# The low-rank result in a tile of its own, not in the masks' scratch buffer

## The chip, the cores and the metric

The kernel runs as one program on one core of a Trainium2 chip. The engines are TensorE (PE, with its weight loads as PEld), VectorE (DVE), ScalarE (ACT), GpSimd (POOL) and SyncE (SP); each takes its own instructions in order, and they wait for each other through semaphores. The metric is the device time of one execution in microseconds (us). Three runs took 1478.11, 1479.92 and 1480.67 us, so the median before is 1479.92 us.

## The reference

One layer of a hybrid encoder, for 256 tokens of 2048 features in float32:

```
u      = rms_norm(x) @ w_in                       # 2048 -> 5408 columns
y_conv = conformer_conv(u[value], u[gate])        # 31 taps, 1024 channels
y_rwkv = rwkv7_time_mix(u[r, k, v, low-rank])     # 16 heads of 64, a recurrence over time
h      = x + concat(y_conv, y_rwkv) @ w_out
out    = rms_norm(h + moe(rms_norm(h)))           # 4 groups of 8 experts, top 1 and then top 2
```

The low-rank columns are the last 288 of w_in (64 for the decay, 64 for a, 160 for the gate). They are shifted by one frame with the mix `mu`, go through tanh or sigmoid, and are then multiplied by small matrices (`w_lora_up`, `a_lora_up`, `g_lora_up`) inside the time mix.

## The kernel before

**Stages.** The program has a front (norm, input projection, convolution, time mix, output projection), a short routing, and an expert stage of 16 pairs of experts, in which 400 MB of expert weights are read. The front keeps features on partitions: the normed input is held as two float32r parts, yh and yl (tiles yha, yhb, yla, ylb), and each 1 MB chunk of w_in, as it lands in the ring of six buffers w, is split on the chip into hi (ACT, line 246) and lo (DVE, line 247), four k-tiles at a time, into three rotating buffers each. A projection of 256 columns is two accumulators acc of 128 columns, and 16 k-tiles of three matmuls each (hi x yh, hi x yl, lo x yh, line 218), so 96 matmuls. The accumulators rotate through a PSUM pool of three banks (`pacc`).

**The beginning.** `norm_in` computes the low-rank columns first, before the norm's scale is known: 32 matmuls (line 314) of x times w_lo fill two banks of `pacc`, tiles la[0] and la[1], one for each half of the tokens. The scale rs is applied when they are evicted (line 376). Meanwhile ytmp, yh and yl are made (lines 342 to 344) and the first three splits. Then `small_loads` and `const_tiles` follow on DVE and POOL: some scaled parameters (lines 192 to 204), and the masks of the time mix, which are built in a scratch tile scr (lines 127 to 171). The scratch has the buffer with the tag "mix" in `ypool`, which has one buffer; ytmp has it before, and the tile mix (the convolution's output, eight blocks of 256 columns) has it after.

**`lora`** evicts la[0] and la[1] on ACT into lt (line 376), transposes three column ranges of each on PE (line 378, six transposes into three banks mm), shifts them (line 361 on ACT, 362 on DVE) into T1, G1 and G2, and applies tanh (lines 384, 386). T1 is first used in `rwkv_decay` and G1, G2 in `rwkv_out`.

**Behind it** stands `conv_duo(0)`: the gate projection (96 matmuls), its tanh sg from the two accumulators (line 645, ACT), the value projection (96 more), and UP = (sg + 1) x value (line 651, DVE), which frees the value's accumulators. Then come the convolution's 31 taps into mix (lines 656, 658), and `rwkv_duo(0)` with its projections of k, r and v. Fills of constant tiles from ident (line 722, ACT; line 719, DVE) stand in the same stretch.

**The order** of each engine's instructions is made by a list scheduler from the order of the code and priorities: loads and splits of a projection have a raised priority, the taps a lowered one. A tile that takes over a buffer waits for all that was done to the tile before it. The expert stage has its order on PE by hand; each weight chunk is loaded by SP (line 1095) when its slot is free.

Of the kernel before, what the change touches and what calls it, by code (L numbers as in the profile page):

```python
# [76 lines left out]
class Block:  # L77
# [293 lines left out]
    def lora(self):  # L371
        nc = self.nc
        ps = [self.bank(self.pmm, [128, 256], "mm") for _ in range(3)]
        for i in range(2):
            lt = self.mix[:, 2 * i:2 * i + 2].rearrange("p a b -> p (a b)")[:, 0:288]
            nc.scalar.activation(lt, self.la[i], AF.Copy, scale=self.rs[:, i:i + 1])
            for p, c in zip(ps, (0, 128, 160)):
                nc.tensor.transpose(p[:, 128 * i:128 * i + 128], lt[:, c:c + 128], self.ident)
        T1 = self.lo.tile([128, 256], F32, name="T1")
        G1 = self.lo.tile([128, 256], F32, name="G1")  # L380
        G2 = self.lo.tile([128, 256], F32, name="G2")
        for i, (p, t) in enumerate(zip(ps, (T1, G1, G2))):
            self.shift(p, self.mul_s[:, i:i + 1], self.omul[:, i:i + 1], t)
        nc.scalar.activation(T1[0:64], T1[0:64], AF.Tanh)
        for t in (G1, G2):
            nc.scalar.activation(t, t, AF.Tanh, scale=0.5)
            nc.vector.tensor_scalar(t, t, 0.5, 0.5, op0=OP.mult, op1=OP.add)
        self.T1, self.G1, self.G2 = T1, G1, G2
        self.tap("T1", T1)
# [902 lines left out]
```

## Time and profile before

| | |
|---|---|
| median of three runs | 1479.92 us |
| the profiled execution, its own time | 1477.63 us |
| its span | 1475.8 us |
| PE busy | 1398.8 us (95%) |
| DVE busy | 654.7 us (44%) |
| ACT busy | 416.1 us (28%) |
| POOL busy | 33.5 us (2%) |
| mean granted TensorE clock | 0.989 |
| DMA | 471.48 MB, mean 319 GB/s |

The span is from the first to the last instruction; the execution's own time is 1.8 us longer. Matmuls overlap, and their ends are modelled, so a busy PE is not a PE at its peak. Shares are means over stages with different limits: the front works on PE, DVE and ACT, the expert stage on PE and the DMA engines.

### The profile page before, as it was taken

The page shows a single profiled execution, that of the slowest core. Times are in us where ns is not written, and L with a number is a line of the kernel's source. Part 1 is how long each engine was busy: PE and PEld are TensorE (multiplying, and loading weights), DVE is VectorE, ACT ScalarE, POOL GpSimd, SP SyncE. Part 2 cuts the span into 40 slices and gives each one's busy share as a digit, 9 for nine tenths or more (in the row PEclk, how much of TensorE's full clock was granted, in tenths as well). Part 3 has the DMA queues.
Part 4 walks back from the last instruction along what each step waited for, and adds up shares of the span by engine and source line. Part 5 has one row for each costly group of instructions (what it writes and reads, how often), then busy time and mean ns, then how long its engine had stood idle before and what let it go on. Part 6 is the DMA issues. An engine that isn't in the chain of part 4 may idle for free.

```text
span 1475.8 us, 21342 instructions
## 1 busy us (share of the span) xinstructions
PE 1398.8 (95%) x8738; PEld 855.4 (58%) x8738; DVE 654.7 (44%) x1343; ACT 416.1 (28%) x770; POOL 33.5 (2%) x66
## 2 busy tenths in 40 slices
PE   6999999999999989999999999999999998999995
PEld 5989888989889954344344344344344343443432
DVE  6797986968967542232232232232231221312314
ACT  5657756676596330010010010000010000000102
POOL 5000000000000000000000000000000000000000
PEclk9999999999999999999999999999999999999997
DMA  7443332432537669999999999999999999999994
GB/s 279 145 150 115 110 131 88 149 118 76 179 129 290 280 250 371 425 424 425 424 422 426 425 424 422 426 424 425 425 424 425 424 426 424 423 426 425 422 424 155
DMA packets 68678, 471.48 MB, mean 319 GB/s; under 512 B 7984, under 2 KB 10096, under 8 KB 13280
## 3 DMA queue, kind: packets, MB, share of 16 engines
q1 hardware_dynamic: 67344, 467.96, 78.1%
q0 software_dynamic: 1088, 2.09, 0.6%
q8 instruction: 71, 1.16, 0.3%
q14 instruction: 31, 0.25, 0.0%
q10 hardware_dynamic: 144, 0.01, 0.0%
HBM read 467.93 MB, written 2.10 MB: 318 GB/s over the span
## 4 chain that ended last, share of the span: by engine, by line
PE 54%; DMA 30%; DVE 10%; ACT 2%; issue 1%; SPq 0%; ACTq 0%; DVEq 0%
DMA w<-in_w_up_dram 20%; PE acc L218 13%; DMA w<-in_w_down_dram 9%; PE y L218 9%; PE g L218 8%; PE u L218 8%; PE mm L218 7%; PE gt L218 5%; DVE lo L247 3%; PE cb L218 3%; DVE mix L658 2%; DVE MB L495 1%; PE cn L218 1%; ACT hi L246 1%; DVE xe L978 1%
## 5 line engine op out<-in xcount | busy, mean ns | idle before, releaser
L218 PE MATMUL u<-w,xe 128*64 128x512 f32 x1024 | 243.8, 593 | 10.8 <-DMA w<-in_w_up_dram 10.5
L218 PE MATMUL g<-w,xe 128*64 128x512 f32 x1024 | 241.3, 598 | 9.9 <-DMA w<-in_w_gate_dram 7.6
L218 PE MATMUL y<-w,hT 128*64 128x512 f32 (+1 forms) x1040 | 232.2, 594 | 0.7 <-ACT hT L1039 0.7
L1056 DVE TENSOR_TENSOR acc<-acc,cb 128x512 f32<-128x512 f32 (+1 forms) x130 | 86.3, 674 | 220.0 <-PE cb L218 220.0
L218 PEld LDWEIGHTS u<-w,xe 128*64 128x64 f32 x1024 | 75.7, 137 | 162.6 <-issue 138.6
L1031 DVE TENSOR_TENSOR hid<-sg,u 128x256 f32<-128x256 f32 x32 | 19.6, 613 | 322.7 <-PE u L218 322.7
L218 PEld LDWEIGHTS g<-w,xe 128*64 128x64 f32 x1024 | 72.0, 137 | 147.8 <-issue 127.2
L218 PEld LDWEIGHTS y<-w,hT 128*64 128x64 f32 x1040 | 70.7, 137 | 134.2 <-issue 118.1
L247 DVE TENSOR_TENSOR lo<-w,hi 128x1024 fp32r<-128x1024 f32 x108 | 127.5, 1180 | 47.0 <-ACT hi L246 34.3
L1027 ACT ACTIVATE sg<-g 128x512 f32<-128x512 f32 x16 | 9.6, 597 | 461.2 <-PE g L218 461.2
L218 PE MATMUL gt<-S,vt 128*128 128x128 f32 x1024 | 126.7, 280 | 6.7 <-DVE xe L978 5.2
L218 PEld LDWEIGHTS gt<-S,vt 128*128 128x128 f32 x1024 | 121.4, 195 | 15.0 <-DVE xe L978 8.7
L246 ACT ACTIVATE hi<-w 128x1024 fp32r<-128x1024 f32 x108 | 110.6, 1025 | 47.4 <-PE acc L218 44.0
L1069 ACT ACTIVATE yh<-y,gate 128x512 fp32r<-128x512 f32 (+1 forms) x65 | 44.3, 681 | 251.6 <-PE y L218 251.6
L658 DVE SCALAR_TENSOR_TENSOR mix<-UP,dw_s,mix 128x256 f32<-128x256 f32 x240 | 103.9, 476 | 2.6 <-ACT mix L656 2.4
L218 PE MATMUL acc<-yha,hi 128*128 128x256 f32 x320 | 92.3, 288 | 0.6 <-DVE rs L362 0.3
L218 PE MATMUL acc<-yla,hi 128*128 128x256 f32 x320 | 92.3, 288 | 0.0
L218 PE MATMUL acc<-yhb,lo 128*128 128x256 f32 x320 | 92.1, 288 | 0.0
L218 PE MATMUL acc<-yha,lo 128*128 128x256 f32 x320 | 91.8, 287 | 0.0
L218 PE MATMUL acc<-ylb,hi 128*128 128x256 f32 x320 | 91.4, 286 | 0.0
L218 PE MATMUL acc<-yhb,hi 128*128 128x256 f32 x320 | 90.4, 283 | 0.0
L978 DVE TENSOR_TENSOR xe<-gt,nffnp_s 128x512 f32<-128x512 f32 (+1 forms) x65 | 44.4, 683 | 85.6 <-PE gt L218 85.5
(354 smaller groups left out, 1907.1 us busy)
## 6 DMA issues: line engine op xcount, KB each, us to landing
w<-in_w_gate_dram SPq DMA_DIRECT2D x128, 1024.0 KB, 19.6
w<-in_w_up_dram SPq DMA_DIRECT2D x128, 1024.0 KB, 19.6
w<-in_w_down_dram SPq DMA_DIRECT2D x126, 1024.0 KB, 19.6
w<-in_w_in_dram SPq DMA_DIRECT2D x40, 1024.0 KB, 5.0
w<-in_w_out_dram SPq DMA_DIRECT2D x8, 768.0 KB, 4.6
w<-in_w_out_dram SPq DMA_DIRECT2D x6, 1024.0 KB, 5.1
xT_s<-in_xT_dram SPq DMA_DIRECT2D x4, 512.0 KB, 6.6
wlast<-in_w_out_dram SPq DMA_DIRECT2D x2, 1024.0 KB, 6.6
```

Of the source, the lines that this page charges most:

```text
L218: self.nc.tensor.matmul(*a, **k)
L246: nc.scalar.activation(hi, view, AF.Copy)
L247: nc.vector.tensor_sub(lo, view, hi.bitcast(F32))
L495: V.copy_predicated(MB[:, 2 * h + c], self.mkP.rearrange("p a b -> p (a b)"), P12[h])
L658: V.scalar_tensor_tensor(c, u, d, c, op0=OP.mult, op1=OP.add)
L978: self.nc.vector.tensor_mul(xe[:, a:a + n], ps, self.nffnp_s[:, k0:k0 + n, None].to_broadcast([128, n, 128]))
L1027: A.activation(sg, gp, AF.Silu)
L1031: V.tensor_mul(hid, *(t.rearrange("s (p f) -> s f p", f=4)[:, f:f + 2] for t in (sg, up)))
L1056: V.tensor_add(a, a, cb)
L1069: A.activation(yh, yp, AF.Copy, scale=gate)
```

## The change

The two evictions of the low-rank result no longer write to slices of mix. Each takes a tile of the tag "tl" in the pool `tmp`, of 128 x 512 floats in two buffers, whose first 288 columns are used. The tag is there already: `rwkv_mats` (line 511) takes tiles of it later for its transposes, by the same helper `lg`.

```diff
         for i in range(2):
-            lt = self.mix[:, 2 * i:2 * i + 2].rearrange("p a b -> p (a b)")[:, 0:288]
+            lt = self.lg("tl", (128, 4, 128)).rearrange("p a b -> p (a b)")[:, 0:288]
             nc.scalar.activation(lt, self.la[i], AF.Copy, scale=self.rs[:, i:i + 1])
```

Every engine has the same instructions as before (ACT's loads of its function tables stand elsewhere); the scheduler puts some of them in another order in the first part of the program, up to the k projection of `rwkv_duo(0)`. POOL's and SP's order is the same.

On PE, before: the end of the gate projection's first accumulator, as far as its splits are there (36 matmuls), the six transposes, and the second accumulator.

```order
L218 MATMUL acc<-yhb,hi 128x256
L218 MATMUL acc<-ylb,hi 128x256
L218 MATMUL acc<-yhb,lo 128x256
L378 MATMUL mm<-ident,mix 128x128 x6
L218 MATMUL acc<-yha,hi 128x256
L218 MATMUL acc<-yla,hi 128x256
L218 MATMUL acc<-yha,lo 128x256
```

On PE, now: the start of the gate projection.

```order
L218 MATMUL acc<-yha,hi 128x256
L218 MATMUL acc<-yla,hi 128x256
L218 MATMUL acc<-yha,lo 128x256
L378 MATMUL mm<-ident,tl 128x128 x3
L218 MATMUL acc<-yha,hi 128x256
L218 MATMUL acc<-yla,hi 128x256
L218 MATMUL acc<-yha,lo 128x256
L218 MATMUL acc<-yha,hi 128x256
L378 MATMUL mm<-ident,tl 128x128 x3
L218 MATMUL acc<-yla,hi 128x256
```

The transposes stood behind 36 gate matmuls, and now stand behind three and seven. The gate's two accumulators, which came one after the other for the first 36 matmuls each, now take turns at every split (12 matmuls each).

On ACT, before: from the last makings of yhb to the eviction of the low-rank result (DT and EP are the constant tiles of line 722).

```order
L343 ACTIVATE yhb<-ytmp 128x512 x4
L722 ACTIVATE DT_267<-ident 128x512
L722 ACTIVATE DT_268<-ident 128x512
L722 ACTIVATE EP_260<-ident 128x512
L722 ACTIVATE EP_261<-ident 128x512
L722 ACTIVATE EP_262<-ident 128x512
L722 ACTIVATE EP_263<-ident 128x512
L722 ACTIVATE EP_264<-ident 128x512
L722 ACTIVATE EP_265<-ident 128x512
L376 ACTIVATE mix<-acc,rs 128x288 x2
```

On ACT, now: from the first of these yhb on.

```order
L343 ACTIVATE yhb<-ytmp 128x512
L376 ACTIVATE tl<-acc,rs 128x288
L343 ACTIVATE yhb<-ytmp 128x512
L376 ACTIVATE tl<-acc,rs 128x288
L343 ACTIVATE yhb<-ytmp 128x512
L246 ACTIVATE hi<-w 128x1024
L343 ACTIVATE yhb<-ytmp 128x512
L722 ACTIVATE DT_267<-ident 128x512
L722 ACTIVATE DT_268<-ident 128x512
L722 ACTIVATE EP_260<-ident 128x512
L246 ACTIVATE hi<-w 128x1024
```

The evictions moved ahead of all eight fills, and the fourth split of the gate's weights and the first of the value's come between the yhb and the fills.

On ACT, before: the stretch from the shifts to the first sg.

```order
L361 ACTIVATE G_379<-mm,omul 128x256
L384 ACT_TABLE_LOAD
L384 ACTIVATE T_377<-T_377 64x256
L246 ACTIVATE hi<-w 128x1024
L386 ACTIVATE G_378<-G_378 128x256
L246 ACTIVATE hi<-w 128x1024
L386 ACTIVATE G_379<-G_379 128x256
L246 ACTIVATE hi<-w 128x1024
L645 ACTIVATE sg<-acc 128x256
```

On ACT, now: the same stretch, from the second to last piece of fills on.

```order
L246 ACTIVATE hi<-w 128x1024
L722 ACTIVATE EP_265<-ident 128x512
L361 ACTIVATE T_379<-mm,omul 128x256
L361 ACTIVATE G_380<-mm,omul 128x256
L361 ACTIVATE G_381<-mm,omul 128x256
L246 ACTIVATE hi<-w 128x1024
L645 ACT_TABLE_LOAD
L645 ACTIVATE sg<-acc 128x256 x2
L246 ACTIVATE hi<-w 128x1024
```

The two sg moved ahead of the tanh of T1, G1 and G2, and the table load stands before them. On DVE the lo of the same splits moved up likewise: one stands between the last two yl, and one each after the memset of line 131, after line 154, after the second piece of line 162 and after the shifts of line 362.

## Rows read from the trace of the kernel before

**Rows 1.** Page, busy tenths in 40 slices: PE.

```profile
PE   6999999999999989999999999999999998999995
```

**Rows 2.** PE's waits, whole span: us in total, times, longest us.

```profile
PE u L218 <- DMA w<-in_w_up_dram: 10.5, 10, 1.3
...
PE mm L378 <- ACT mix L376: 7.3, 1, 7.3
```

**Rows 3.** Busy time by stretch: PE, PEld, DVE, ACT, POOL; clock, DMA share, GB/s.

```profile
32.00:39.28 7.28, 0.00 (x0) 0.00 (x1) 6.75 (x39) 4.45 (x10) 4.39 (x14) 0.82 0.30 123
39.28:43.60 4.32, 4.32 (x21) 4.32 (x22) 1.39 (x4) 3.48 (x7) 0.00 (x0) 0.51 0.00 0
43.60:60.00 16.40, 16.40 (x141) 16.40 (x141) 9.08 (x10) 8.35 (x11) 0.00 (x0) 1.00 0.56 193
60.00:100.00 40.00, 38.67 (x313) 35.71 (x311) 39.37 (x83) 23.92 (x39) 2.14 (x4) 1.00 0.48 165
100.00:450.00 350.00, 339.10 (x3003) 308.57 (x3005) 284.26 (x556) 242.09 (x465) 9.66 (x18) 1.00 0.36 122
...
600.00:1000.00 400.00, 397.58 (x2022) 174.87 (x2022) 104.31 (x206) 28.07 (x43) 0.00 (x0) 1.00 1.01 424
```

**Rows 4.** Timeline of ACT, 26 to 80 us: start, us, instruction, idle before.

```profile
26.96 1.23 ACT L343 ACTIVATE yhb<-ytmp 128x512 fp32r<-128x512 f32 x2 [1.89 <-DVE ytmp L342]
...
32.69 3.21 ACT L722 ACTIVATE EP<-ident 128x512 f16<-128x512 f32 x6
38.73 0.89 ACT L376 ACTIVATE mix<-acc,rs 128x288 f32<-128x288 f32 x2 [2.83 <-DVE w L171]
40.43 0.47 ACT L361 ACTIVATE T<-mm,omul 128x256 f32<-128x256 f32 x1 [0.81 <-PE mm L378]
...
41.66 1.28 ACT L384 ACT_TABLE_LOAD   x1
...
43.27 1.04 ACT L246 ACTIVATE hi<-w 128x1024 fp32r<-128x1024 f32 x1
...
47.79 0.39 ACT L645 ACTIVATE sg<-acc 128x256 f32<-128x256 f32 x1 [0.47 <-PE acc L218]
```

**Rows 5.** Timeline of DVE, 26 to 80 us.

```profile
29.80 0.67 DVE L342 TENSOR_TENSOR ytmp<-y1a,mm 128x512 f32<-128x512 f32 x1
...
32.43 0.16 DVE L192 TENSOR_SCALAR omul<-mul_s 128x3 f32<-128x3 f32 x1
...
33.88 0.11 DVE L132 MEMSET scr<- 64x64 f32 x1
...
36.45 0.28 DVE L156 TENSOR_TENSOR scr<-scr 128x128 f32<-128x128 int32 x1
...
37.86 0.48 DVE L165 TENSOR_TENSOR mkB<-scr 128x128 uint8<-128x128 f32 x2
...
44.35 1.23 DVE L247 TENSOR_TENSOR lo<-w,hi 128x1024 fp32r<-128x1024 f32 x1 [2.14 <-ACT hi L246]
...
60.51 0.42 DVE L651 SCALAR_TENSOR_TENSOR UP<-sg,acc 128x256 f32<-128x256 f32 x1 [0.29 <-PE acc L218]
```

**Rows 6.** Timeline of PE, 0 to 110 and 31.5 to 100 us.

```profile
25.75 2.10 PE L314 MATMUL acc<-w,y1b 128*128 128x288 f32 x8
...
39.28 1.54 PE L378 MATMUL mm<-ident,mix 128*128 128x128 f32 x6 [7.33 <-ACT mix L376]
40.48 0.56 PE L218 MATMUL acc<-yha,hi 128*128 128x256 f32 x1
...
41.05 0.41 PE L218 MATMUL acc<-yha,lo 128*128 128x256 f32 x1
41.26 0.41 PE L218 MATMUL acc<-yha,hi 128*128 128x256 f32 x1
```

**Rows 7.** Waits of SP's DMA queue, 440 to 620 us.

```profile
SPq L1095 <- PE g L218: 39.2, 6, 13.2
SPq L1095 <- PE y L218: 20.7, 4, 10.4
```

## The prediction

> **What bounds the kernel now.** I read the page's slices first: TensorE (PE) is busy nine tenths or more in nearly every slice but the first [rows 1], so what matters in the front is where PE stands still. The list of PE's waits has one long wait there: the six transposes of line 378 wait 7.3 us, once, for the eviction of line 376. The waits for expert weights sum to more, but they are many short ones, the longest 1.3 us [rows 2]. The busy time by stretch shows what that one wait costs: from 32.0 to 39.28 us PE runs nothing while VectorE (DVE) is busy 6.75 of 7.28 us. Then from 39.28 to 43.6 PE's granted clock is 0.51, its 1.2 GHz level, and from 43.6 on it is 1.00, 2.4 GHz; PE had idled before it fell, and had worked again for 4.3 us before it rose [rows 3]. ScalarE (ACT) tells why: the eviction at 38.73 had stood 2.83 us behind DVE's tile w, line 171 [rows 4], the last instruction of the mask building. The lora tile was a slice of mix, mix takes over scr's buffer, and so the eviction had to wait for every mask. PE could not pass it by: two of the three acc banks held the low-rank result, and the second half of the first projection needs one of them.
>
> After 60 us PE and DVE are both nearly full up to 100 us (38.67 and 39.37 of 40), PE stays so to 450 us (339.1 of 350) at clock 1.00, and the expert stage runs on the DMA engines (share 1.01 at 424 GB/s from 600 to 1000) [rows 3].
>
> **The change, step by step.** The bytes, the instructions and the DMAs are the same; only the target of two evictions differs. The wait for the masks goes, and the scheduler then puts the two evictions behind the first and second yhb on ACT, the transposes between the first gate matmuls on PE, and the splits hi and lo (lines 246, 247) between the memsets and masks. Nothing moves on the queues of GpSimd and SyncE. From the k projection on, all engines have the same order as before, so the question is when that part begins. I take as its mark the second UP write on DVE (line 651), which waits for PE's last value matmul: 60.51 us before [rows 5].
>
> What is late next. I follow the new order with the old durations. The first yhb ends at 26.96 + 0.62 = 27.6, and the last eight low-rank matmuls end at 25.75 + 2.10 = 27.85, those of the first half about 0.25 earlier [rows 4, 6]. The evictions take 0.50 each with a yhb of 0.62 between them, so they end near 28.1 and 29.2. PE has three gate matmuls to do, waits about 0.2 for the first, and again about 0.2 for the second: 0.4 in all. The six transposes took from 39.28 to 40.5 at the half clock, so 0.1 each at the full one, and by 29.5 they are done with seven of the 96 gate matmuls. A matmul costs 16.40 / 141 = 0.116 us at the full clock [rows 3]; the other 89 end at 29.5 + 10.3 = 39.8.
>
> Then 23 value matmuls run into the bank of low-rank half two, until 42.5, and the 24th wants a bank that line 645 (sg) must free. ACT reaches that late: yhb at 30.5 behind its ytmp (29.80 + 0.67), hi at 31.5 when PE has done the first 24 gate matmuls, then yhb (0.6), three fills of line 722 at 3.21 / 6 = 0.53, hi (1.0), four fills, hi, one fill, the three shifts (40.43 to 41.66, 1.2), hi, the table load (1.28), sg (0.39): 31.5 + 1.05 + 0.6 + 1.6 + 1.0 + 2.1 + 1.0 + 0.5 + 1.2 + 1.05 + 1.28 + 0.39 = 43.3 [rows 4, 5]. PE waits 0.8 us there, where it now waits nothing. The remaining 73 value matmuls end at 43.3 + 8.5 = 51.8, with the drain of the last 52.1. Behind the waiting PE stand only these matmuls, and DVE and ACT wait for them.
>
> DVE's splits must be there in time, since each now stands behind a piece of mask work. The pieces last 32.43 to 33.9, to 36.45 and to 37.9 (1.4, 2.6 and 1.4 us); the last has 0.8 to 38.6 and then five instructions, two fills and three shifts, at about the 0.4 of a UP, 2.8 in all [rows 5]. With 1.23 for each lo, the four lo of the value projection end near 37.1, 40.9, 43.5 and 47.5, and PE wants them at 40.0, 41.4, 46.2 and 49.0: 2.9, 0.5, 2.7 and 1.5 us to spare. The second is the tight one.
>
> The sum:
> - the idle stretch: 7.3 us gone;
> - the half clock behind it: 1.2 GHz for 4.32 us costs (1 - 0.51) x 4.32 = 2.1 at most, and 14 matmuls at 0.21 instead of 0.116 cost 1.3 at least [rows 3, 6]. The transposes lie in that stretch too, so I take 1.9;
> - the two short waits for the evictions: -0.4;
> - the new wait for sg: -0.8.
>
> That is 8.0; the walk by itself gives 60.5 - 52.1 = 8.4. I take 8.2 us.
>
> Bounds, since nothing here was ever run in this order. Above: DVE's work between 32 and 60 us is 6.75 + 1.39 + 9.08 = 17.2 of 28 us [rows 3], so it can be squeezed by 10.8 us and no more. Below: if the mask work, from the second piece on (33.9 to the eviction at 38.73, 4.8 us) [rows 4, 5], were all to stand in the way of splits that PE waits for, 3.4 us would be left. I stay by the walk, whose spare times come from the nearest rows.
>
> Does the shift last to the end? What follows waits only for engines. SyncE's waits before expert weights are for PE and DVE to free slots (39.2 and 20.7 us on lines of PE are the largest) [rows 7], DMA has 0.36 of its time in use up to 450 us [rows 3], and the expert stage is so many bytes at one rate from its first free slot. So it starts 8.2 us earlier and ends 8.2 us earlier. On the profiled execution, 1477.63 us, that is 1469.4; the median of the runs is 2.3 us above it, and from 1479.92 I forecast 1471.7 us.
>
> A page speaks against the clock term. The Trainium skill, "TensorE: Matmul & The Clock Gate", section "A second HAM failure mode: psum-queue depth-cycling", says that short idles between matmul groups that cycle through PSUM banks can make the clock swing between its two levels. By that rule the new bank wait would bring back some of the 1.9 us or more; it is the third rival below. The trace bears it out little: between 100 and 450 us, where matmul groups share the same banks, the granted clock is 1.00.
>
> **Rivals.**
> - Masks in the way. If the lo with 0.5 us to spare is late, and those behind it too, PE waits for DVE instead of ACT. For it: a piece of mask work now stands ahead of each of these splits, and DVE takes its queue in order. Against it: DVE has 10.8 us idle in that stretch. It gives a gain of 3 to 5 us, 1475 to 1477.
> - Swallowed later. If the expert weights came from a stream that started by itself, an earlier front would only wait for them: 1479.9. For it: the DMA share of 1.01. Against it: the waits of rows 7 are all for engines. That the change doesn't free the eviction at all would give the same time; against that stands the order, in which the transposes come behind three gate matmuls instead of 36.
> - Slower, by the clock. If the many short waits between 27 and 52 us held PE at 1.2 GHz, the 192 matmuls of the first two projections would take 0.21 instead of 0.116: 192 x 0.094 = 18 us more, less the 7.3 + 1.9 that went, so 9 us slower, 1489. It decides from 8.2 / 0.094 = 87 matmuls at the half clock on. For it: the clock did fall once after PE stood still here. Against it: it fell in a stand of 7.3 us, and the new waits are 0.2 to 0.8.
>
> **How the numbers follow.** The forecast with gains of 5 to 10.8 us has 0.82; masks in the way 0.07; swallowed, or not done, 0.07; slower by the clock 0.04. A difference under 0.2% (3 us) can hardly be told from none here. Faster by more takes the forecast and most of the second, 0.88; within it 0.08; slower 0.04. The range runs from a gain of 10.8 us (1469.1) with a little of the runs' own spread (1478.11 to 1480.67), 1468.6, to 3.7 us, 1476.2; that leaves out the two last rivals and the weaker part of the masks' one.
>
> **What would show it.** In the changed profile the wait of line 378 for line 376 falls from 7.3 us to under 0.5; no stretch between 27 and 60 us has a granted clock of 0.5; PE waits near 42 us for sg, 0.4 to 1.2 us; the second UP write comes at 52 us; the first copies into MB and the first expert matmul come 8 us earlier, and the expert stage has its old length. It is wrong if PE waits for lo between 40 and 49 us, if the clock shows its lower level after 30 us, or if the shift at UP has shrunk by the time the expert stage ends.

## The result and the profile after

The first comparison gave 1468.93 us (four runs, 1466.81 to 1469.90) against 1479.99 us (four runs) on the same chip: ratio 0.9925, 95% interval 0.9908 to 0.9943. Two more comparisons of the same pair, told below, gave 0.9952 (0.9938 to 0.9965) and 0.9943 (0.9930 to 0.9956). By the ratios the three are 11.1, 7.1 and 8.4 us, and their intervals overlap; the forecast was a gain of 8.2 us, to 1471.7. The profiled execution took 1469.9 us with a span of 1467.9, against 1477.63 and 1475.8: 7.7 to 7.9 us. Why these numbers differ is the second half of this text. One reason lies in the kernel before: in the 57 executions of it in the later comparisons the median is 1477.0 us, and the four of the first comparison (1478.11 to 1480.67) all lie at the upper end of that spread (1475.23 to 1480.16), while the changed kernel's medians of the first and third comparison differ by 0.4 us only. Of the 57, all that took 1478 us or more had a mean granted clock of 0.986 or 0.987, and all under 1477.8 had 0.989 or 0.990. So some 3 us of the 11.1 most likely come from those four executions, and not from the change.

The page's slices of PE. The first digit has risen from 6 to 8; one other digit differs, that of the slice with the routing, which reads 7 for 8 [rows 1].

```profile
PE   8999999999999979999999999999999998999995
```

PE's waits over the whole span: us in total, times, longest. The wait of line 378 is no longer in the list [rows 2]; the new wait for sg is its last line. The waits for expert weights are what they were.

```profile
PE u L218 <- DMA w<-in_w_up_dram: 10.7, 9, 1.6
...
PE acc L218 <- ACT sg L645: 0.2, 1, 0.2
```

Busy time by stretch: PE, PEld, DVE, ACT, POOL; clock, DMA share, GB/s. The later stretches begin 8 us earlier than those of [rows 3], as the forecast would have them.

```profile
27.00:32.00 5.00, 5.00 (x43) 4.83 (x42) 4.33 (x6) 3.04 (x7) 5.00 (x10) 1.00 0.95 362
32.00:39.28 7.28, 7.28 (x64) 7.28 (x63) 6.61 (x25) 7.28 (x15) 4.64 (x12) 1.00 0.59 225
39.28:43.60 4.32, 4.10 (x35) 3.90 (x34) 4.32 (x18) 3.29 (x6) 0.12 (x1) 1.00 0.54 154
43.60:52.00 8.40, 8.40 (x73) 7.94 (x72) 7.13 (x16) 5.20 (x8) 0.00 (x0) 1.00 0.61 196
52.00:92.00 40.00, 37.37 (x308) 34.86 (x306) 39.66 (x83) 23.77 (x40) 2.15 (x4) 1.00 0.47 162
92.00:442.00 350.00, 340.04 (x3014) 309.26 (x3012) 283.72 (x555) 242.44 (x466) 9.69 (x18) 1.00 0.36 122
592.00:992.00 400.00, 397.58 (x2021) 174.81 (x2022) 104.05 (x206) 27.62 (x42) 0.00 (x0) 1.00 1.01 424
```

From 32.00 to 39.28 PE did nothing before and is now busy all the time; DVE builds the same masks in it. From 39.28 to 43.60 the clock is 1.00 where it was 0.51.

ACT, the stretch of the evictions and of sg (start, us, instruction, idle before). The evictions stand at 26.97 and 27.87 instead of 38.73, and the first sg (the tanh of the gate projection) at 41.94 [rows 4].

```profile
26.97 0.49 ACT L376 ACTIVATE tl<-acc,rs 128x288 f32<-128x288 f32 x1
27.35 0.62 ACT L343 ACTIVATE yhb<-ytmp 128x512 fp32r<-128x512 f32 x1
27.87 0.49 ACT L376 ACTIVATE tl<-acc,rs 128x288 f32<-128x288 f32 x1
...
40.65 1.28 ACT L645 ACT_TABLE_LOAD   x1
41.94 0.66 ACT L645 ACTIVATE sg<-acc 128x256 f32<-128x256 f32 x2
```

DVE, with the four lo of the value projection and the UP writes [rows 5]. The rs of line 331 is a mark that lies ahead of the change: it was at 17.79 before, so 0.5 us of every shift of a start below come from an earlier beginning of this one execution. The last row is the third UP write.

```profile
17.27 0.17 DVE L331 RECIPROCAL rs<-rs 128x2 f32<-128x2 f32 x1 [3.71 <-ACT rs L330]
...
35.38 1.23 DVE L247 TENSOR_TENSOR lo<-w,hi 128x1024 fp32r<-128x1024 f32 x1
...
39.24 1.21 DVE L247 TENSOR_TENSOR lo<-w,hi 128x1024 fp32r<-128x1024 f32 x1
...
41.80 1.21 DVE L247 TENSOR_TENSOR lo<-w,hi 128x1024 fp32r<-128x1024 f32 x1
...
45.57 1.21 DVE L247 TENSOR_TENSOR lo<-w,hi 128x1024 fp32r<-128x1024 f32 x1
...
50.44 0.96 DVE L651 SCALAR_TENSOR_TENSOR UP<-sg,acc 128x256 f32<-128x256 f32 x2
...
131.23 0.42 DVE L651 SCALAR_TENSOR_TENSOR UP<-sg,acc 128x256 f32<-128x256 f32 x1 [0.73 <-PE acc L218]
```

The same two marks in the trace of the kernel before:

```profile
17.79 0.17 DVE L331 RECIPROCAL rs<-rs 128x2 f32<-128x2 f32 x1 [4.11 <-ACT rs L330]
...
140.54 0.42 DVE L651 SCALAR_TENSOR_TENSOR UP<-sg,acc 128x256 f32<-128x256 f32 x1 [0.73 <-PE acc L218]
```

PE: the transposes stand in two threes among the first gate matmuls, and the only idle time that is left before the second UP is 0.22 us for sg [rows 6].

```profile
27.60 0.52 PE L378 MATMUL mm<-ident,tl 128*128 128x128 f32 x3
...
28.44 0.53 PE L378 MATMUL mm<-ident,tl 128*128 128x128 f32 x3
...
42.38 0.39 PE L218 MATMUL acc<-yha,hi 128*128 128x256 f32 x1 [0.22 <-ACT sg L645]
```

SP's waits before expert weights, 440 to 620 us, are still for PE to free slots [rows 7].

```profile
SPq L1095 <- PE g L218: 45.1, 8, 13.9
SPq L1095 <- PE y L218: 20.7, 4, 10.4
```

**Where the time went.** Two marks split the span. From rs to the third UP write (line 651; 140.54 before, 131.23 after) it is the front: 122.75 us before, 113.96 after, 8.8 less. From there to the last accumulation of line 1056 (1462.35 and 1455.14) it is the rest: 1321.8 before, 1323.9 after, 2.1 more. The shift is 9.3 us at the first copy into MB (97.10 to 87.79) and still 9.3 when ACT loads the function table for the experts' silu (line 1027, 536.30 to 527.01). It is 8.95 at the first expert matmul (538.91 to 529.96), 8.6 at the first silu itself (572.20 to 563.56) and 7.2 at the end. In the changed kernel:

```profile
527.01 1.28 ACT L1027 ACT_TABLE_LOAD   x1
...
563.56 0.60 ACT L1027 ACTIVATE sg<-g 128x512 f32<-128x512 f32 x1 [35.27 <-PE g L218]
```

The table load is only a mark of the routing's end; the expected text of the run with the routing filled, further down, counts it as a silu and so calls the first silu the second. The longer waits of PE there are alike in both traces; what differs is the clock, as the runs below show.

### The profile page after: what moved, and what is told of

The parts are those of the page before. It is cut to its first block, busy times and chain, and to the rows that moved or that the text cites. A ratio compares the mean times of both kernels' runs of the same rounds, so it can differ in the third digit from the quotient of the medians.

```text
span 1467.9 us, 21346 instructions
## 1 busy us (share of the span) xinstructions
PE 1398.4 (95%) x8738; PEld 854.9 (58%) x8738; DVE 654.4 (45%) x1343; ACT 415.5 (28%) x770; POOL 34.5 (2%) x66
## 4 chain that ended last, share of the span: by engine, by line
PE 58%; DMA 26%; DVE 11%; ACT 3%; issue 1%; ACTq 0%; SPq 0%; DVEq 0%
DMA w<-in_w_up_dram 18%; PE acc L218 12%; PE y L218 10%; PE g L218 9%; PE u L218 9%; DMA w<-in_w_down_dram 8%; PE mm L218 7%; PE gt L218 6%; DVE lo L247 3%; PE cb L218 3%; DVE mix L658 2%; DVE MB L495 1%; PE acc L314 1%; ACT hi L246 1%; PE cn L218 1%
```

## Experiments

Each front below is the time from rs to the third UP write in that run's trace, so that the start of the program is set equal; each shift is against the 122.75 us of before. Each ratio is against executions of the kernel before on the same chip.

**The pair again.** Without an edit.

> The changed kernel once more, against the kernel before on the same chip, in five rounds. The single pair of traces gave 7.7 to 7.9 us, the medians of the first runs 11.1 us with an interval of 8.4 to 13.6. Theory A (the gain is the front's shift at the second UP write, 9.5 us in the first trace, less what the granted clock gives back later, which differs from execution to execution): a gain between 7 and 10 us, and in the new trace UP again near 51 us, the first expert matmuls some 9 us earlier, and stretches at clock 0.5 in the expert stage that need not lie where they lay. Rival B (the changed kernel also gains something in the expert stage that one trace does not show): a gain of 10 us or more, and the last expert pair earlier by more than UP is.

1470.81 against 1477.29 us, ratio 0.9952 (0.9938 to 0.9965), 7.1 us. Front 113.85, shift 8.9; the rest 1323.8. Theory A: the gain is in the front, and the stretches at half clock near 523 and 1400 us are there again.

**The wait kept, the tile new.**

```diff
-        V.tensor_scalar(w8, jj[:, 0:8], -1.0, 8.0, op0=OP.mult, op1=OP.add)
+        self.masks = V.tensor_scalar(w8, jj[:, 0:8], -1.0, 8.0, op0=OP.mult, op1=OP.add)
...
-            nc.scalar.activation(lt, self.la[i], AF.Copy, scale=self.rs[:, i:i + 1])
+            ev = nc.scalar.activation(lt, self.la[i], AF.Copy, scale=self.rs[:, i:i + 1])
+            self.after(ev, self.masks)
```

> The lora tile keeps its own buffer, but its two evictions are made to wait for the last mask instruction (tile w, line 171), as they did before. Theory A (the wait for the masks is the whole cause): no difference from the kernel before, 1478 to 1481 us, the eviction at 38.7, PE's wait of line 378 at 7.3 us, a stretch at clock 0.5 behind it and the second UP write at 60 us. Rival B (the other buffer itself matters, because mix's later users now need not wait for the transposes): 2 us or more of the gain stay, UP at 58 or earlier.

1478.80 us, ratio 1.0007 (0.9998 to 1.0016). PE waits 7.4 us for line 376, the front takes 122.71 us: shift 0.0. The new buffer alone is worth nothing; theory A.

```profile
PE mm L379 <- ACT tl L376: 7.4, 1, 7.4
```

**Only a short wait, on cent (line 134).** The same edit with self.masks at line 134.

> As the run before, but the evictions wait only for cent (line 134), an early piece of the mask building, which ends near 34.8 us; they stand behind all fills on ACT, which end near 35.9. So PE should stand still for 3.5 to 4.5 us instead of 7.3. This separates the two terms of the forecast, idle and clock. If the clock falls only after the long stand: it stays at 1.00 behind this one, the gain is 2.8 to 3.8 of idle and the 1.9 of the clock, 4.7 to 5.7 us, 1474 to 1475 us, the second UP write near 55 us. If the clock falls behind this stand too: 2.8 to 3.8 us alone, 1476 to 1477 us, UP near 57, and a stretch at 0.5 between 37 and 45 us.

1474.01 us, ratio 0.9978 (0.9965 to 0.9991). The run turned out to be another than planned. ACT's rows show that the eviction did not wait for cent at all (cent was done at 33.4 us): it follows the fills without idle time.

```profile
31.26 3.21 ACT L723 ACTIVATE EP<-ident 128x512 f16<-128x512 f32 x6
34.37 0.87 ACT L376 ACTIVATE tl<-acc,rs 128x288 f32<-128x288 f32 x2
```

So this is the case without a wait but with ACT's old order. PE stood 4.5 us, and the clock fell even so (0.72 in the 10 us behind the stand). Of the two cases the second came, and smaller than expected: shift 1.8 us. The median alone, 3.3 us under before, would have pointed to the first case; the trace decides.

**The scratch moved, the tile left in mix** (against the kernel before).

```diff
-        scr = self.ypool.tile([128, D], F32, tag="mix", name="scr")
+        scr, scr2 = (self.mp.tile([128, 6, 256], F32, tag=t, name=t + "scr").rearrange("p a b -> p (a b)")
+                     for t in ("m0a", "m1a"))
...
-        ge = ts([128, 5, 128], F32, "ge")
+        ge = scr2[:, 0:640].rearrange("p (a b) -> p a b", a=5)
```

> The kernel before, in which the masks' scratch gets buffers of its own (two that the output projection uses later), and the lora tile stays in mix. The wait for the masks is gone by another way, and the scheduler leaves ACT's evictions behind the eight fills. In the run with the short stand the eviction did not wait for cent at all, but came straight behind the fills, so that run was already this case. Theory A (the wait alone is worth little, and most of the gain comes from the evictions' new place in ACT's and PE's order): the eviction straight behind the fills, PE's stand of line 378 at 4 to 5 us, the third UP write (line 651) 1.5 to 2.5 us earlier than before with the program's start set equal, and 1473 to 1476 us. Rival B (the other buffer is what counts): 2 us or more better or worse than that.

1475.97 us, ratio 0.9984 (0.9974 to 0.9995). The evictions are behind the fills, PE stands 4.5 us, the shift is 3.6 us where 1.5 to 2.5 were expected.

```profile
PE mm L379 <- ACT mix L377: 4.5, 1, 4.5
```

This run and the one with the short wait have the same stand and differ by 1.7 us; the clock behind it differs too, as the rows below show. What follows: of the 7.3 us of idle time 2.8 go with the wait for the masks alone, and 4.5 stay as long as the evictions stand behind the fills on ACT; the run with the short wait has the new tile and still these 4.5. And the new order does not follow from the end of that wait alone: here the masks are out of the way, and the scheduler left the evictions behind the fills. The tile in mix still takes over the buffer of ytmp, whose last user, a yl, ended at 31.8 us, after the first fills had begun at 30.9. That this is why the order stayed is likely, but no run shows it.

**The stand filled with work.** Twelve matmuls in front of the transposes of the kernel before; the eviction still waits.

```diff
...
+        for _ in range(12):
+            self.after(nc.tensor.matmul(ps[0], self.ident, self.xt(0), start=True, stop=True), self.small)
```

> The kernel before, in which PE gets twelve matmuls of its own in front of the six transposes of line 378 (ident times a tile of x, 128x256 in float32, their result is overwritten by the transposes); they wait for tile omul only (line 192, ended near 32.6 us) and should run to about 38 us. The eviction still waits for the masks, so the idle term stays and only the clock term can go. Theory A (PE standing still is what brings the clock down, and the half clock costs PE time): clock 1.00 between 32 and 50 us, transposes at 38.7 to 39.3 as before, the second UP write 1.5 to 2.5 us earlier than before when the program's start is set equal, a median 1 to 2.5 us under before. Rival B (the half clock cost nothing, since PE then waits for splits anyway): UP at its old place, no difference. In the run with the short stand the stretch at 0.5 was the same length and began 3.7 us into the stand, and it cost more, since more of it lay behind the stand.

1474.00 us, ratio 0.9986 (0.9976 to 0.9997). The transposes are at 37.85, with rs at 16.36: no earlier than before (21.5 us behind it in both). The clock stays at 1.00. The second UP, the mark of the prediction, is 1.2 us earlier, less than the 1.5 to 2.5 expected, and the third is 2.2 us earlier. That is not the clock by itself: PE now waits for a split that was there in time before,

```profile
43.55 0.39 PE L218 MATMUL acc<-yha,hi 128*128 128x256 f32 x1 [0.21 <-ACT hi L246]
```

and between the second and the third UP it stands 2.6 us in all (stands over 0.1 us) where it stood 3.4 before, since the scheduler's order differs a little. So what the clock is worth by this run lies between 1.2 and 2.2 us.

The 10 us behind the stand, by the columns of the busy time above (the clock is third from the right), one row each of before, of the kept wait, of the short wait, of the moved scratch and of the filled stand:

```profile
39.28:49.28 10.00, 10.00 (x69) 10.00 (x70) 5.45 (x9) 7.51 (x13) 0.00 (x0) 0.79 0.26 87
```

```profile
38.27:48.27 10.00, 10.00 (x73) 10.00 (x74) 5.22 (x9) 7.72 (x13) 0.00 (x0) 0.84 0.26 89
```

```profile
35.00:45.00 10.00, 10.00 (x64) 10.00 (x65) 7.90 (x25) 7.21 (x12) 0.17 (x1) 0.72 0.28 99
```

```profile
35.70:45.70 10.00, 10.00 (x75) 10.00 (x76) 8.11 (x26) 8.01 (x13) 0.17 (x1) 0.86 0.30 95
```

```profile
37.85:47.85 10.00, 9.78 (x78) 9.12 (x79) 5.95 (x11) 8.22 (x14) 0.00 (x0) 1.00 0.30 99
```

One minus the clock, times ten, is the work lost: 2.1, 1.6, 2.8, 1.4 and 0 us. With the idle time saved (0, 0, 2.8, 2.8 and 0) the shifts should be 0, 0.5, 2.1, 3.5 and 2.1; measured were 0, 0.0, 1.8, 3.6 and 2.2 at the third UP, and 0, 0.4, 2.2, 3.6 and 1.2 at the second. The sum of the two terms holds to half a us, but for the filled stand at the second UP, where 0.9 is missing. It also misses in a later trace with the full stand, that of the kernel before with both edits below: there 3.0 us are lost, so it should be 0.9 us later than before, and its third UP is 0.35 later.

```profile
37.75:47.75 10.00, 10.00 (x63) 10.00 (x64) 5.38 (x9) 7.31 (x12) 0.00 (x0) 0.70 0.26 89
```

A smaller thing is left open: from 30 to 40 us behind rs, with the clock at 1.00, matmuls of the same form start every 118 ns in the traces of before, of the kept wait, of the short wait and of the moved scratch, and every 113 ns in those of the filled stand and of this last one. Over 100 matmuls that is half a us. Among the traces of the changed kernel both values occur, so it is not the order of the instructions, and no row says where it comes from.

**One half evicted early, the other late.**

```diff
-            lt = self.lg("tl", (128, 4, 128)).rearrange("p a b -> p (a b)")[:, 0:288]
+            lt = (self.lg("tl", (128, 4, 128)) if i == 0 else self.mix[:, 2:4]).rearrange("p a b -> p (a b)")[:, 0:288]
```

> Only the first half of the tokens is evicted to the new tile; the second half stays in mix and waits for the masks. Theory C (what PE lacks is one of the three acc banks; a single one set free lets both gate accumulators run): PE does all 96 gate matmuls during the mask building, and the value projection's second accumulator finds a bank after the late eviction at 38 to 39 us: a gain of 7 to 9.5 us, second UP write at 51 to 53 us, no clock of 0.5 between 27 and 60 us. Rival D (PE takes its instructions in order, and the second half's transposes stand in front of gate matmuls, as the six did before): PE waits for line 376 for several us even so, and 0 to 4 us are gained, UP at 56 us or later.

1470.75 us, ratio 0.9956 (0.9942 to 0.9970), shift 7.5 us, clock 1.00 from 27 to 60. Theory C: one bank set free is most of it. The second eviction even came later than before, and PE waited only 0.8 us for it and 1.2 for sg:

```profile
43.29 0.50 ACT L376 ACTIVATE mix<-acc,rs 128x288 f32<-128x288 f32 x1 [2.15 <-DVE w L171]
```

**The later clock.** Two edits on the changed kernel. The first gives PE ten matmuls in the routing:

```diff
...
+        warm = self.bank(self.pmm, [128, 256], "mm")
+        for _ in range(10):
+            self.after(self.mm(warm, self.ident, self.xt(15), start=True, stop=True), self.last, sync=False)
         rk = self.bank(self.pmm, [128, 2, 32], "mm")
```

> The changed kernel with ten matmuls (ident times a tile of the residual, result not used) for PE during the routing, where it stands still for 5.4 us for DVE's tile Mb and where the clock is then at its lower level as the expert stage starts. Theory A (the front's shift shrank there from 9.3 to 8.7 us because the half clock fell differently on the first gate matmuls): clock 1.00 from 515 to 535 us, the stretch from the routing's end to the second expert silu 1 to 2.5 us shorter than in the changed kernel's trace (there 36.5 us), and 1 to 2.5 us off the total, since the expert stage is carried through at one rate. Rival B (the DMA engines' rate alone sets that stage): the stretch shorter, but the gain gone by the last expert pair. Rival C: the dummies are late and delay the routing, 0 to 1 us slower.

1467.13 us, ratio 0.9934 (0.9919 to 0.9950). In the stretch below (the changed kernel, then this run) the clock is 1.00 instead of 0.66, and from the table load of line 1027 to the first silu it takes 34.7 us instead of 36.5. Theory A; the gain of 1.9 us is still there at the fifteenth of the sixteen silus. At the last accumulation it is 3.4 us, but the part behind the fifteenth silu goes with the clock near 1400 us (0.91 instead of 0.83), which this edit does not touch.

```profile
520.70:530.70 10.00, 4.67 (x21) 3.95 (x23) 7.61 (x45) 3.27 (x6) 0.00 (x0) 0.66 0.55 228
```

```profile
520.70:530.70 10.00, 8.68 (x50) 6.09 (x50) 8.28 (x46) 3.14 (x5) 0.00 (x0) 1.00 0.61 227
```

The second spreads the last norm's gain over the partitions by matmuls of 128 input rows, of which all but one are zero:

```diff
-        self.nfr = self.fin[0][0:1, :]
-        self.nc.gpsimd.dma_start(self.nfr, self.nfin)
-        self.one_row = self.fin[1][0:1, 0:128]
+        self.nfr = self.fin[0]
+        self.nc.gpsimd.memset(self.nfr, 0.0)
+        self.nc.gpsimd.dma_start(self.nfr[0:1, :], self.nfin)
+        self.one_row = self.fin[1][:, 0:128]
```

> The changed kernel with the matmuls that spread the last norm's gain over the partitions (line 1111) on 128 input rows instead of one: the row's tile is set to zero first and all its rows are multiplied by ones. Theory A (the clock falls near 1400 us, though PE is busy 100%, because these matmuls use one row of the array): no stretch at 0.5 between 1395 and 1412 us, these matmuls 3.8 us instead of 5.2, the last expert pair 2 to 3.5 us earlier against the first ones than in the changed kernel's trace, and a median 1.5 to 3.5 us lower. Rival B (it falls for another cause, such as float32 weights loaded often in that place): the same stretch at 0.5 and no gain.

1465.66 us, ratio 0.9924 (0.9909 to 0.9940). PE's rows in the changed kernel and then in this one: 1*128 has become 128*128, the eight take 3.69 us instead of 5.24, and the sixteen behind them 2.04 instead of 3.78. That is nearly all the clock: in the trace of before, where it fell only behind these matmuls, the eight with one row took 3.79 us (third fence).

```profile
1398.84 5.24 PE L218 MATMUL gt<-fin,fin 1*128 1x512 f32 x8
1404.01 3.78 PE L218 MATMUL gt<-S,vt 128*128 128x128 f32 x16
```

```profile
1397.81 3.69 PE L218 MATMUL gt<-fin,fin 128*128 128x512 f32 x8
1401.33 2.04 PE L218 MATMUL gt<-S,vt 128*128 128x128 f32 x16
```

```profile
1407.64 3.79 PE L218 MATMUL gt<-fin,fin 1*128 1x512 f32 x8
```

The stretch around them, of the changed kernel and of this run; PE is busy for all 20 us in both, yet the clock is 0.83 in one and 1.00 in the other:

```profile
1391.25:1411.25 20.00, 20.00 (x76) 8.93 (x74) 3.01 (x5) 2.39 (x4) 0.00 (x0) 0.83 1.01 425
```

```profile
1391.25:1411.25 20.00, 20.00 (x93) 8.25 (x90) 2.05 (x4) 2.39 (x4) 0.00 (x0) 1.00 1.01 424
```

Theory A; from the fifteenth silu to the last accumulation it takes 89.2 us instead of 93.5, 4.3 less and so more than the 3.5 expected; the clock also stayed up near 1432 us.

**Both edits.**

> Both edits of the two runs before on top of the changed kernel. If both theories A hold: 2.5 to 6 us under the changed kernel, 0.9915 to 0.9935 of the time before, and less spread from execution to execution than the changed kernel shows (4.3 us). If both rivals B hold: as the changed kernel, 0.9952.

1464.68 us, ratio 0.9915 (0.9901 to 0.9928), five runs between 1464.01 and 1465.04. By the ratios it is faster than both kernels, and its spread is smaller; the three kernels on one chip, next, say the same.

**Three kernels on one chip:** the kernel before with both edits, the changed one with both, and the changed one.

> The kernel before with the two edits that keep the clock up later (matmuls in the routing, the last norm's gain on 128 rows), and its lora tile still in mix. Beside the same two edits with the changed lora tile this measures the change with little of the later clock in it. Theory A (the front's shift of 8.9 us is carried to the end, and only the later clock gives parts of it back or not): 1472.5 to 1474.5 us, and 8.3 to 9.5 us between the two, with both spreads under 2 us but for the stretch at half clock in the front. Rival B (a part is lost in the expert stage for another reason, since that is bound by the DMA engines): 7.5 us or less between the two.

> The changed kernel with the two edits that keep the clock up later, once more, on the same chip as the run before and the run behind this one. Theory A: 1464 to 1465.5 us, 0.9910 to 0.9925 of before, 4 to 6 us under the changed kernel and 8.3 to 9.5 us under the kernel before with the same two edits. Rival: on this chip the dips of the clock fall elsewhere, and the two edits gain under 3 us.

> The changed kernel once more, on the same chip as the two runs before. Theory A: 7 to 9 us under the kernel before (the front's 8.9 us less what the later clock gives back in the mean), 1467 to 1471 us with a spread of 3 to 5 us between executions, and the stretches at half clock near 523 and 1400 us in its trace. Rival: the difference from before comes out at 10 us or more, as in the first comparison, and then something besides the front gains.

They took 1473.50, 1464.90 and 1468.57 us, with ratios of 0.9973 (0.9964 to 0.9981), 0.9921 (0.9908 to 0.9934) and 0.9943 (0.9930 to 0.9956) against before. With both edits the change is worth 8.6 us: theory A. The two edits gain 3.7 us on the changed kernel, so a little less than the 4 expected. The third comparison's 8.4 us and these 8.6 agree. The first kernel's runs spread over 3.3 us, more than expected: the stretch at half clock behind its stand is not always the same (0.70 in its trace, 0.79 in that of before; its front is 0.35 us longer).

All fronts of the changed order lie between 113.85 and 114.11 us (seven traces), while the rest moves with the granted clock at three places. The clocks are those of the stretches 515 to 545 (routing), 1395 to 1415 (the spreading of the gain) and 1420 to 1445 us (last pair). In before and the kept wait the lower level lasts beyond 1415 us, so that their second column shows too little of it:

| kernel | routing | gain | last pair | the rest, us |
|---|---|---|---|---|
| before | 0.89 | 0.93 | 0.93 | 1321.8 |
| after, first trace | 0.89 | 0.83 | 0.93 | 1323.9 |
| after, second | 0.89 | 0.83 | 0.93 | 1323.8 |
| after, third | 0.89 | 0.91 | 1.00 | 1321.3 |
| wait kept | 0.83 | 0.88 | 0.93 | 1324.5 |
| short wait | 0.89 | 0.91 | 0.93 | 1321.9 |
| moved scratch | 0.83 | 0.83 | 0.93 | 1324.8 |
| filled stand | 0.89 | 0.91 | 1.00 | 1320.6 |
| one half early | 0.89 | 0.91 | 0.93 | 1322.0 |
| with the routing filled | 1.00 | 0.91 | 0.93 | 1320.5 |
| with 128 gain rows | 0.89 | 1.00 | 1.00 | 1319.3 |
| both, first | 1.00 | 1.00 | 1.00 | 1318.0 |
| both, second | 1.00 | 1.00 | 0.93 | 1319.2 |
| before with both | 1.00 | 1.00 | 1.00 | 1317.6 |

Summed over the three places, the clock was at its lower level for 0 us in the two traces with the shortest rest (1317.6 and 1318.0) and for 20.5 us in the two with the longest (1324.5 and 1324.8).

## Why the prediction was right, and where its terms were off

- **The wait and the order.** Right: the wait is the cause (kept, it takes the whole gain away), and without it the new tile lets the scheduler put the evictions ahead of the fills. The prediction did not say that this order is the larger part; 4.5 of the 7.3 us hang on it.
- **The idle stretch, 7.3.** Right; it is gone whole.
- **The half clock, 1.9.** About right: 2.1 by the clock's row, the upper bound that the prediction gave, and 1.2 to 2.2 by the run with the filled stand. By the row there was nothing to take off for the transposes.
- **The two waits for the evictions, -0.4.** PE's list has none between 27 and 53 us. The evictions came nearly as worked out (ends at 27.46 and 28.36, against 28.1 and 29.2 less the 0.5 of the earlier start), and PE was still busy then.
- **The wait for sg, -0.8.** Mis-sized: it is 0.2, under the 0.4 to 1.2 that was to show it. ACT's table load began at 40.65, and by my chain at 41.6 less 0.5; 0.4 too much in a chain of ten terms.
- **The splits.** The four lo end near 36.6, 40.5, 43.0 and 46.8, against 37.1, 40.9, 43.5 and 47.5: nearly all of that is the earlier start. PE has no wait for a lo in its list, so the masks were not in the way.
- **The sum.** 8.0 to 8.4 was worked out to the second UP. That came at 50.98, 51.5 with the start set equal, against 52.1: a shift of 9.0, which is 7.3 and 2.1 less 0.2, within 0.2 us. At the third UP it is 8.8 (8.6 to 8.9 in seven traces). So the mechanism was right, and the two waits, taken 1.0 us too long, are most of the difference.
- **To the end.** This step failed in part: "the expert stage is so many bytes at one rate from its first free slot" holds between the first silu and the fifteenth (798.0 to 798.7 us in all fourteen traces), but not at its two ends. There the time moves with PE's clock, which differs from execution to execution. In the profiled pair 2.1 us were given back, so that one of the signs of being wrong, a shift at UP that has shrunk by the end, did come; in the third trace 0.5 more were gained. The median of 1468.93 lies 2.8 us under the forecast, and most of that is where the forecast started: from 1479.92 us, the median of three executions, where 57 later ones have 1477.0.
- **The rivals.** The third rival's rule (the Trainium skill, "TensorE: Matmul & The Clock Gate", section "A second HAM failure mode: psum-queue depth-cycling") would have brought half clock where groups share banks and PE stops shortly. The trace does not show it: the clock is 1.00 in all rows from 27 to 442 us. Before the second UP it was hardly put to the test, with one stand of 0.22 us. Swallowed later would have needed a stage that starts by itself; the first expert matmul moved by 8.95 us. That the change frees nothing is ruled out by the wait that is gone.

## What to carry to other kernels

A buffer that is shared for space alone makes its next user wait for the last instruction on the buffer, and in a kernel with a list scheduler that wait also moves what is ordered around it; look for what the scheduler will do once it is gone, since that can be the larger part (here 4.5 of 7.3 us). Price a stand of PE with the clock behind it. And measure a change in the front by marks in the trace that lie around it: the marks agreed to 0.3 us where executions of the same kernel differed by 3 to 5.

## What was not expected of the hardware

The granted clock fell near 1400 us while PE was busy 20.00 of 20 us by the profile. What ran there were eight float32 matmuls of one input row. In all ten traces with one row the clock fell there, during these matmuls or at most 1.3 us behind the last of them; with 128 rows it did not fall in the three traces that have them on the changed kernel, nor in that on the kernel before. Whether the zero rows or only their number counts was not tried.

After equal stands of 4.5 us the clock of the next 10 us was 0.72 in one program and 0.86 in another (the lower level lasted 5.7 us into them, and 2.7), and after stands of 7.3 to 7.4 us it was 0.79, 0.84 and 0.70: the price of a stand is not fixed by its length. What sets it stays open.
